# One layer of a hybrid decoder on one Trainium2 core: the output projection's weight units in another order, two weight splits and a norm chain moved

## The chip, the cores and the metric

The kernel runs on 1 core of one Trainium2 chip. The metric is device time in microseconds (us). Engines are named as the profile names them: PE is TensorE's matmul and PEld its weight load, DVE is VectorE, ACT is ScalarE, POOL is GpSimd, SP is SyncE, which here only issues loads.

## The reference, cut to what matters

For 512 tokens of width 1024 in float32, one layer does three things, each between two RMS norms:

```
x = x + 0.5 * rms_norm(swiglu(rms_norm(x, ffn1_pre_g), ffn1_w_gu, ffn1_w_down), ffn1_post_g)
y = hybrid_mixer(rms_norm(x, mix_pre_g), w_in, conv_w, ..., w_o)
x = x + rms_norm(y, mix_post_g)
x = x + 0.5 * rms_norm(swiglu(rms_norm(x, ffn2_pre_g), ffn2_w_gu, ffn2_w_down), ffn2_post_g)
```

The mixer ends in the place that the change touches:

```
y_lru  = rg_lru(x_lru, ...) * gelu(gate_lru)            # 512 channels: recurrence
y_attn = sliding_window_sink_attention(q, k, v, sinks)  # 512 channels: attention
y = concatenate([rms_norm(y_lru, g_lru_out), rms_norm(y_attn, g_attn_out)], axis=-1)
return y @ w_o                                          # w_o is 1024 x 1024
```

## The kernel before, in words

**Products in parts.** Each float32 operand is split into a high part (rounded, ACT: `whi`, `yah`, `ylh`) and a low part (the rest, DVE: `wlo`, `yal`, `yll`). A product is high by high, high weight by low operand, and low weight by high operand.

**Order.** The tile framework keeps the order in which the code issues work, engine by engine. It places the waits and chooses the buffers, PSUM banks among them; each engine runs its own list in order.

**Weights.** The class `Weights` holds all weights as units in one order. A raw tile (1 MB, five of them, two held by `x_rows` here) is loaded by SP and holds several units. `W.take` hands out the next unit. `W.fill(n)` makes sure that n units past those taken are split: for each a cast on ACT (L184) and a subtraction on DVE (L189). When a raw tile's last unit is split, the next load is issued. The code that calls `W.fill` thus sets where the casts and splits stand in the two engines' lists. One unit of `w_o`, the pair (6, 1), is split by a `deferred` call earlier on.

**The output projection.** A unit of `w_o` is a pair of contraction chunks (128 channels each) by one half `dh` of the 1024 outputs: (4, 0), (6, 0), (4, 1), (6, 1) for attention and (0, 0), (2, 0), (0, 1), (2, 1) for the recurrence, in that order before. The tokens are four blocks `tb` of 128, each with two PSUM banks, `wo00` to `wo31` (block, half). The attention part comes first, for blocks 0 to 2: `yah0` to `yah3` and `yal0` to `yal3` are the parts of its four channel chunks. They come from the transposes `atp0` to `atp3` (L1577), which stand in PSUM banks too. For n = 0 and 1 only the high operand is multiplied; then come the low ones of both.

**The gating.** In between stand the statistics of the recurrence: `acc_lru`, the sum of squares on DVE, goes through PE (L454), ACT (`rms_slru`) and DVE (`dg_lru`) and is spread by PE (L469). ACT copies it out (`bc`), and for each of four chunks DVE scales `xc`, ACT makes `ylh` and DVE `yll`. Behind them all stand four casts and splits of recurrence weights. PE does the third block of attention and block 3 meanwhile, and then the recurrence part block by block in `boundary`, through `produce(tb, dh)`.

**The boundary.** In `boundary`, `rows.piece` takes the sum of squares of a finished bank (ACT `sqyr`, L602) and multiplies it by the gain (DVE `zr`, L624). `rows.steps` is a block's norm chain, which `advance` takes a step further at a time: DVE adds the sums (`toty`), ACT and DVE invert, DVE adds to `x_rows`, ACT squares (`sqxr`), DVE adds (`totx`), and so on to the normed `xn`, which PE transposes into `tp_r` (L650). Between these, `W.fill` splits the first units of the next feed-forward, `bg` and `bu`.

Of the kernel before, what the change touches and what calls it, by code (L numbers as in the profile page):

```python
# [15 lines left out]
P = 128  # L16
T = 512
# [6 lines left out]
KC = C // P  # L24
# [98 lines left out]
def tile_layer(ctx: ExitStack, tc: tile.TileContext, out: bass.AP, **ins: bass.AP):  # L123
    nc = tc.nc
    pe, dve, act, pool, sync = nc.tensor, nc.vector, nc.scalar, nc.gpsimd, nc.sync
# [15 lines left out]
    def bank(name):  # L141
        return psum.tile([P, T], F32, tag="bank", name=name)

    def t2k(name, dt=F32):
        return big.tile([P, T], dt, tag="t2k", name=name, bufs=NT2K)

    def wt(name, w=T, dt=F32):
        return tmp.tile([P, w], dt, tag="w", name=name, bufs=NW)


    W = Weights()
    w1, w2, w_in, w_o = ins["ffn1_w_gu"], ins["ffn2_w_gu"], ins["w_in"], ins["w_o"]

    def load_raw(srcs, nk, w, name):
        raw = wpool.tile([P, nk * w], F32, tag="raw", name=f"raw_{name}", bufs=NRAW).rearrange("p (k c) -> p k c", k=nk)
        o = 0
        for src in srcs:
            n = src.shape[1]
            sync.dma_start(raw[:, :, o:o + n], src.rearrange("(k p) c -> p k c", p=P))
            o += n  # L160
        return raw
# [16 lines left out]
    def add_unit(r, part, nk, c, name, low=dve):  # L178
        def two(t, like):
            return t.rearrange("p k (i d) -> p k i d", i=2) if len(like.shape) == 4 else t  # L180

        def cast(raw):
            x, (hi, lo) = part(raw), w_tiles(nk, c, name)
            act.copy(two(hi, x), x)  # L184
            return hi, lo

        def take_low(raw, hi, lo):
            x = part(raw)
            low.tensor_sub(two(lo, x), x, two(hi.bitcast(F32), x))  # L189

        W.unit(r, cast, take_low)
# [132 lines left out]
    for c in (0, 2):  # L324
        for add in add_cols(w_in, KC + c, KD, "gt"):
            add()
    WO = [(k, dh) for k0 in (KC, 0) for dh in range(2) for k in (k0, k0 + 2)]
    for k0 in (KC, 0):
        for dh in range(2):
            r = W.raw(lambda k0=k0, dh=dh: load_raw([w_o[0, k0 * P:(k0 + 4) * P, dh * T:(dh + 1) * T]], 4, T, f"wo{k0}{dh}"))  # L330
            for i in (0, 2):
                add_unit(r, lambda raw, i=i: raw[:, i:i + 2, :], 2, T, f"wo{k0 + i}{dh}", deferred if (k0 + i, dh) == (KC + 2, 1) else dve)
    GROUPS2 = [(0, 6), (6, 10), (10, 14), (14, 18), (18, 22)]
    add_layer(w2, ins["ffn2_w_down"], "b", GROUPS2, CLASSIC2, SEVEN_DOWN2, 0)
# [14 lines left out]
    for i in range(2):  # L349
        load_x(0, i)  # L350
        for o in (0, F):
            r = first_raw[o, i] = t2k(f"first{o}{i}").rearrange("p (k c) -> p k c", k=4)
# [43 lines left out]
    def col(name, i):  # L396
        return colrange(name)[:, i:i + 1]
# [24 lines left out]
    def k_high(ws, banks, xs, sl, ks):  # L422


        for k in ks:
            xh = xs[k][0][:, sl]
            for (hi, lo), ps in zip(ws, banks):
                pe.matmul(ps[:, sl], hi[:, k, :], xh, start=k == 0, stop=False)
                pe.matmul(ps[:, sl], lo[:, k, :], xh, start=False, stop=False)

    def k_low(ws, banks, xs, sl):
        n = len(xs)
        for (hi, lo), ps in zip(ws, banks):
            for k in range(n):
                pe.matmul(ps[:, sl], hi[:, k, :], xs[k][1][:, sl], start=False, stop=k == n - 1)


    def square(src, sl, name, scale=1.0):
# [40 lines left out]
    def x_high(x, src, gain, sl):  # L479
        act.activation(x[0][:, sl], src, AF.Copy, scale=gain)  # L480
# [175 lines left out]
    def boundary(rows, produce, parts, turns, fills, ahead, name):  # L656


        nxt = rows.nxt
        lower, upper = range(4), range(4, KD)  # L660
        chain = iter(())

        def advance(n):
            for _ in range(n):
                next(chain, None)

        for tb in range(NB - 1):
            for dh in range(2):
                ps = produce(tb, dh)
                for t in turns.get((tb, dh), ()):  # L670
                    rows.turn(t)
                W.fill(fills.get((tb, dh), 0))
                if dh == 0:
                    advance(3)
                rows.piece(tb, dh, ps, parts and parts[tb, dh])
            chain = rows.steps(tb)
            if tb < NB - 2:
                advance(ahead)
        ps = [produce(NB - 1, dh) for dh in range(2)]
        advance(1)  # L680
        rows.turned(nxt.high, 0, lower)
        advance(1)
        rows.turned(nxt.low, 0, lower)
        W.cast(1)
        rows.turned(nxt.high, 0, upper)
        advance(1)
        rows.turned(nxt.low, 0, upper)
        W.fill(2)
        advance(1)
        for dh in range(2):  # L690
            rows.piece(NB - 1, dh, ps[dh], parts and parts[NB - 1, dh])
        if nxt.xg:
            rows.turned(nxt.keep, 0, range(KD))
        xs, (l, r) = nxt.xs, HALF
        W.cast(4)
        ws, banks = [], []

        def one(n, part, xpart, stop=False):
            for w, b in zip(ws[n:], banks[n:]):
                for k in range(KD):  # L700
                    pe.matmul(b[:, l], w[part][:, k, :], xs[k][xpart][:, l], start=k + part + xpart == 0, stop=stop and k == KD - 1)  # L701

        def more():
            ws.extend(W.take(0) for _ in range(2))
            banks.extend(bank(f"{name}n{len(banks)}") for _ in range(2))

        more()
        one(0, 0, 0)
        one(0, 0, 1)
        one(0, 1, 0, True)  # L710
        chain = rows.steps(NB - 1)
        advance(4)
        W.fill(2)
        rows.turn(2)
        more()
        one(2, 0, 0)
        one(2, 0, 1)
        rows.turn(3)
        for cs in (lower, upper):
            rows.turned(nxt.high, 1, cs)  # L720
            rows.turned(nxt.low, 1, cs)
        if nxt.xg:
            rows.turned(nxt.keep, 1, range(KD))
        one(2, 1, 0, True)
        W.fill(2)
        k_high(ws, banks, xs, r, range(KD))
        k_low(ws, banks, xs, r)
        return banks

# [279 lines left out]
    banks = [bank(f"a_first{i}") for i in range(4)]  # L1009
# [228 lines left out]
    def produce(tb, dh):  # L1238
        if dh == 0:
            last_banks[tb] = [bank(f"yal{tb}{i}") for i in range(2)]  # L1240
        if tb or not dh:
            for i, f in last.steps(tb, (dh,) if tb else (0, 1)):
                mm3_out(last_banks[tb][i], hs[f - f0], tb, last.weights(f, i), f % 2, ALL, f == f0, f == f1 - 1)
        if (tb, dh) == (0, 1):
            split_gates()
        return last_banks[tb][dh]
# [56 lines left out]
    k0 = const.tile([P, P], F32, name="k0")  # L1303
# [309 lines left out]
    rows2 = Rows("r2", x_rows, "mix_post_g", 1.0 / D, eps, n2)  # L1613
    wo_banks, wo = [], {}
# [10 lines left out]
    def wo_bank(tb):  # L1625
        wo_banks.append([bank(f"wo{tb}{dh}") for dh in range(2)])

    for tb in range(NB - 1):
        wo_bank(tb)
    for n, (k0, dh) in enumerate(WO[:4]):  # L1630
        wo[k0, dh] = W.take(0)
        for xp in ((0,), (0,), (0, 1), (0, 1))[n]:
            for tb in range(NB - 1):
                wo_product(tb, dh, k0, k0 == KC, False, (xp,))
        if n == 1:
            W.fill(2)
            for k0, dh in WO[:2]:
                for tb in range(NB - 1):
                    wo_product(tb, dh, k0, False, False, (1,))
            for l in lrms:  # L1640
                l.stats()
        if n == 2:
            bc = wt("bc")
            for l, sl in zip(lrms, HALF):
                act.copy(bc[:, sl], l.spread())
            for ci in range(KC):
                dve.tensor_mul(hl[ci], hl[ci], bc)
                y = t2k(f"ylh{ci}", F32R), t2k(f"yll{ci}", F32R)
                x_high(y, hl[ci], col("g_lru_out", ci), ALL)
                x_low(y, hl[ci], col("g_lru_out", ci), ALL)  # L1650
                ysp[ci] = y
            W.fill(3)
    wo_bank(NB - 1)
    for k0, dh in WO[:4]:
        wo_product(NB - 1, dh, k0, k0 == KC, False)
    W.fill(4)

    def produce(tb, dh):
        for k0 in (0, 2):
            if (k0, dh) not in wo:  # L1660
                wo[k0, dh] = W.take(0)
            wo_product(tb, dh, k0, False, k0 == 2)
        return wo_banks[tb][dh]

    banks = boundary(rows2, produce, None, {(2, 0): [0], (2, 1): [1]}, {(0, 1): 1, (1, 0): 2}, 2, "m")

    x_hbm = hbm.tile([T, D], F32, name="x_hbm")
    for tb in range(NB):
# [20 lines left out]
    for tb in range(NB):  # L1689
        end = tb == NB - 1  # L1690
        pieces = [(0, 0, T)] + ([(1, 0, T // 2), (1, T // 2, T)] if end else [(1, 0, T)])
        banks = [bank(f"ybl{tb}{i}") for i in range(len(pieces))]
# [3 lines left out]
        for i, f in last.steps(tb, range(len(pieces))):  # L1696
            dh, c0, c1 = pieces[i]
# [17 lines left out]
        rs = small.tile([P, 1], F32, tag="rs1", name=f"rs_b{tb}")  # L1715
# [34 lines left out]
```

## Time and profile before

| | us |
|---|---|
| median of 3 runs (865.73 to 866.11) | 865.96 |
| the profiled execution | 866.93 |
| its span, first to last instruction | 865.0 |
| PE busy | 853.3 |
| DVE busy | 652.7 |
| ACT busy | 529.8 |

The profiled execution is 1.93 us longer than its span, and 0.97 above the median of the runs. The mean clock granted to TensorE is 0.997 of full speed. In the span, the output projection runs from 465 to 516 us.

A row of the timeline gives the start, the length, the engine, the line, the operation with output and inputs, the shape, how often it stands there, and in brackets how long the engine had been idle before it and what ended that. Several alike are one row, whose length then covers them all. Rows of before have the lines of the code shown above.

### The profile page before, as it was taken

How to read it: one execution, taken by the hardware profiler on the slowest of the kernel's cores; microseconds unless marked ns; L12 is line 12 of the kernel's file. 1: busy time of each engine (PE TensorE's matmuls, PEld its weight loads, DVE VectorE, ACT ScalarE, POOL GpSimd, SP SyncE). 2: the span in 40 equal slices, each digit the busy share in tenths (PEclk: the TensorE clock that was granted, in tenths of full speed). 3: DMA queues.
4: the chain of work that ended last, by engine and by line, in shares of the span. 5: the costliest groups of instructions: out<-in, count | busy, mean ns of one | idle time of the engine just before them, and what ended most of it. 6: DMA issues, size and time to landing. Idle time of an engine off the chain costs nothing.

```text
span 865.0 us, 14200 instructions
## 1 busy us (share of the span) xinstructions
PE 853.3 (99%) x5554; PEld 778.3 (90%) x5554; DVE 652.7 (75%) x894; ACT 529.8 (61%) x905; POOL 168.1 (19%) x202
## 2 busy tenths in 40 slices
PE   8999999999999999999999999999999999999996
PEld 8988999989989998998787779888999998998995
DVE  4988897887898866855688675456589798889856
ACT  6647567566576564755787476335456666657552
POOL 2022005013034011013354021001001402303402
PEclk9999999999999999999999999999999999999999
DMA  8265339739469363143211118235323955938922
GB/s 245 99 195 195 128 106 229 196 95 237 132 122 282 125 216 98 54 142 98 87 37 49 51 48 292 75 119 197 126 90 101 236 155 132 233 99 187 262 89 97
DMA packets 92866, 124.42 MB, mean 144 GB/s; under 512 B 5824, under 2 KB 62464, under 8 KB 92800
## 3 DMA queue, kind: packets, MB, share of 16 engines
q1 hardware_dynamic: 76240, 86.68, 31.8%
q0 software_dynamic: 16416, 36.71, 19.1%
q8 instruction: 43, 0.70, 0.3%
q14 instruction: 23, 0.19, 0.1%
q10 hardware_dynamic: 144, 0.13, 0.0%
HBM read 93.10 MB, written 30.41 MB: 143 GB/s over the span
## 4 chain that ended last, share of the span: by engine, by line
PE 92%; DVE 3%; ACT 2%; POOL 1%; DMA 1%; issue 1%; SPq 0%; DVEq 0%; ACTq 0%
PE aa L819 12%; PE ab L819 11%; PE da L819 6%; PE db L819 5%; PE ba L819 3%; PE bb L819 3%; PE wo L1623 2%; PE a_first L1014 2%; PE mn L701 1%; PE an L701 1%; PE yal L1148 1%; PE yal L1146 1%; PE yb L1148 1%; PE yb L1147 1%; PE yal L1147 1%; PE yb L1146 1%
## 5 line engine op out<-in xcount | busy, mean ns | idle before, releaser
L927 POOL DMA_DIRECT2D yp_b<-stage x42 | 36.5, 1115 | 149.1 <-ACT stage L924 140.3
L927 POOL DMA_DIRECT2D yp_a<-stage x42 | 37.0, 1126 | 146.2 <-ACT stage L924 141.1
L1175 POOL DMA_DIRECT2D yp_b<-stage x8 | 4.3, 541 | 91.8 <-ACT stage L1174 91.0
L1146 PE MATMUL yal<-whi_ad,hha 128*128 128x512 f32 x48 | 18.9, 393 | 0.0
L1148 PE MATMUL yal<-whi_ad,hla 128*128 128x512 f32 x48 | 18.7, 390 | 0.0
L1147 PE MATMUL yal<-wlo_ad,hha 128*128 128x512 f32 x48 | 18.7, 389 | 0.0
L1146 PE MATMUL yb<-whi_bd,hhb 128*128 128x512 f32 x48 | 18.7, 389 | 0.0
L1147 PE MATMUL yb<-wlo_bd,hhb 128*128 128x512 f32 x48 | 18.7, 389 | 0.0
L1148 PE MATMUL yb<-whi_bd,hlb 128*128 128x512 f32 x48 | 18.7, 389 | 0.0
L189 DVE TENSOR_TENSOR wlo_bd<-raw_bd,whi_bd 128x1024 fp32r<-128x1024 f32 x10 | 12.1, 1223 | 8.1 <-ACT whi_bd L184 8.1
L1297 POOL TENSOR_TENSOR xcl<-xc,xch 128x512 fp32r<-128x512 f32 x4 | 6.3, 1570 | 57.1 <-ACT xch L1296 57.1
L189 DVE TENSOR_TENSOR wlo_ad<-raw_ad,whi_ad 128x1024 fp32r<-128x1024 f32 x10 | 12.2, 1221 | 4.0 <-ACT whi_ad L184 4.0
L552 POOL TENSOR_TENSOR xg_f<-xh_f,xl_f 128x256 f32<-128x256 f32 x8 | 5.8, 760 | 46.6 <-DVE xl_f L483 46.6
L409 PE MATMUL gt<-xh_mx,whi_gt 128*128 128x512 f32 x32 | 14.2, 443 | 0.0
L1623 PE MATMUL wo<-whi_wo,yah 128*128 128x512 f32 x32 | 13.1, 410 | 0.8 <-ACT yah L480 0.8
L602 ACT ACTIVATE sqxr<-x_rows 128x512 f32<-128x512 f32 x16 | 10.0, 631 | 5.7 <-DVE x_rows L632 5.7
L1623 PE MATMUL wo<-wlo_wo,ylh 128*128 128x512 f32 x32 | 12.6, 393 | 0.8 <-DVE wlo_wo L189 0.8
L1147 PE MATMUL ybl<-wlo_bd,hhb 128*128 128x512 f32 (+1 forms) x36 | 13.2, 366 | 0.0
L1146 PE MATMUL ybl<-whi_bd,hhb 128*128 128x512 f32 (+1 forms) x36 | 13.2, 366 | 0.0
L1148 PE MATMUL ybl<-whi_bd,hlb 128*128 128x512 f32 (+1 forms) x36 | 13.2, 365 | 0.0
L1709 POOL TENSOR_TENSOR yp_b<-yp_b,grow 128x512 f32<-128x512 f32 x6 | 7.7, 1290 | 27.2 <-ACT ysq L1702 27.2
L1702 ACT ACTIVATE ysq<-yp_b 128x512 f32<-128x512 f32 (+1 forms) x9 | 5.2, 583 | 12.4 <-DVE yp_b L1701 11.7
(1845 smaller groups left out, 3726.5 us busy)
## 6 DMA issues: line engine op xcount, KB each, us to landing
yp_a<-stage POOLq DMA_DIRECT2D x50, 256.0 KB, 7.2
yp_b<-stage POOLq DMA_DIRECT2D x50, 256.0 KB, 8.0
raw_ad<-in_ffn_w_down SPq DMA_DIRECT2D x4, 1024.0 KB
raw_wo<-in_w_o SPq DMA_DIRECT2D x4, 1024.0 KB, 5.1
raw_bd<-in_ffn_w_down SPq DMA_DIRECT2D x4, 1024.0 KB
xn<-in_x SPq DMA_DIRECT2D x8, 256.0 KB, 3.6
x_rows<-in_x POOLq DMA_DIRECT2D x4, 512.0 KB, 12.2
yp_a<-yp_a POOLq DMA_DIRECT2D x8, 256.0 KB, 9.2
```

The costliest lines, as they stand in the source:

```text
L189: low.tensor_sub(two(lo, x), x, two(hi.bitcast(F32), x))
L409: pe.matmul(ps, hi[:, k, :], xh, start=start, stop=False)
L602: act.activation(wt(f"sq{name}{self.name}{tb}{dh}"), src, AF.Square, accum_out=self.ss[name, tb][:, dh:dh + 1])
L701: pe.matmul(b[:, l], w[part][:, k, :], xs[k][xpart][:, l], start=k + part + xpart == 0, stop=stop and k == KD - 1)
L819: pe.matmul(o, w[:, k, js], x, start=first and i + j + k == 0, stop=k == 3 and i == 2, skip_group_check=True)
L927: pool.dma_start(o, st.rearrange("p (a b) -> p a b", a=2) if len(o.shape) == 3 else st, accum_op=ALU.add)
L1014: pe.matmul(banks[j][:, HALF[0]], ws[j][part][:, k, :], n1.xs[k][xpart][:, HALF[0]], start=k == 0 and part == xpart, stop=stop and k == KD ...
L1146: pe.matmul(ps, hh[:, blk], hi[:, k, cs], start=start, stop=False)
L1147: pe.matmul(ps, hh[:, blk], lo[:, k, cs], start=False, stop=False)
L1148: pe.matmul(ps, hl_[:, blk], hi[:, k, cs], start=False, stop=stop)
L1623: pe.matmul(wo_banks[tb][dh], x, w[:, k, :], start=start and k == 0 and w is hi and not xp, stop=stop and k == 1 and xp == 1)
L1709: pool.tensor_mul(y, y, grow[dh][:, c0:c1])
```

## The change

Four things. The units of `w_o` go by pairs of chunks and then by halves: (4, 0), (4, 1), (6, 0), (6, 1), (0, 0), (0, 1), (2, 0), (2, 1). The two units split behind the gating at n = 2 are split ahead of it, behind the statistics at n = 1. In `boundary`, the fill follows `advance` and `rows.piece`, and the first fill is that of (0, 0) instead of (0, 1). And in `k_high` and `k_low` the first matmul of a second half no longer carries the start flag.

```diff
-    WO = [(k, dh) for k0 in (KC, 0) for dh in range(2) for k in (k0, k0 + 2)]
+    WO = [(k, dh) for k in (KC, KC + 2, 0, 2) for dh in range(2)]
     for k0 in (KC, 0):
-        for dh in range(2):
-            r = W.raw(lambda k0=k0, dh=dh: load_raw([w_o[0, k0 * P:(k0 + 4) * P, dh * T:(dh + 1) * T]], 4, T, f"wo{k0}{dh}"))
-            for i in (0, 2):
+        rs = [W.raw(lambda k0=k0, dh=dh: load_raw([w_o[0, k0 * P:(k0 + 4) * P, dh * T:(dh + 1) * T]], 4, T, f"wo{k0}{dh}")) for dh in range(2)]
+        for i in (0, 2):
+            for dh, r in enumerate(rs):
                 add_unit(r, lambda raw, i=i: raw[:, i:i + 2, :], 2, T, f"wo{k0 + i}{dh}", deferred if (k0 + i, dh) == (KC + 2, 1) else dve)
...
             for (hi, lo), ps in zip(ws, banks):
-                pe.matmul(ps[:, sl], hi[:, k, :], xh, start=k == 0, stop=False)
-                pe.matmul(ps[:, sl], lo[:, k, :], xh, start=False, stop=False)
+                for w in (hi, lo):
+                    pe.matmul(ps[:, sl], w[:, k, :], xh, start=False, stop=False, skip_group_check=True)
...
-                W.fill(fills.get((tb, dh), 0))
                 if dh == 0:
                     advance(3)
                 rows.piece(tb, dh, ps, parts and parts[tb, dh])
+                W.fill(fills.get((tb, dh), 0))
...
             for l in lrms:
                 l.stats()
+            W.fill(4)
         if n == 2:
...
                 ysp[ci] = y
-            W.fill(3)
...
-    banks = boundary(rows2, produce, None, {(2, 0): [0], (2, 1): [1]}, {(0, 1): 1, (1, 0): 2}, 2, "m")
+    banks = boundary(rows2, produce, None, {(2, 0): [0], (2, 1): [1]}, {(0, 0): 2, (1, 0): 2}, 2, "m")
```

On PE, at the end of the first pass of attention (the four rows for block 2 of unit (4, 0)) and into the second, before. `whi_wo40` is the high part of unit (4, 0), and the brackets name the engine that a row waits for:

```order
L1623 MATMUL wo20_5312<-whi_wo40_4601,yah0_5228 128x512 [waits PE_49]
L1623 MATMUL wo20_5312<-wlo_wo40_4602,yah0_5228 128x512
L1623 MATMUL wo20_5312<-whi_wo40_4601,yah1_5235 128x512
L1623 MATMUL wo20_5312<-wlo_wo40_4602,yah1_5235 128x512
L1623 MATMUL wo00_5308<-whi_wo60_4761,yah2_5246 128x512 [waits Activation_49]
L1623 MATMUL wo00_5308<-wlo_wo60_4762,yah2_5246 128x512
L1623 MATMUL wo00_5308<-whi_wo60_4761,yah3_5254 128x512 [waits Activation_49]
```

And after:

```order
L1623 MATMUL wo20_5312<-whi_wo40_4601,yah0_5228 128x512 [waits PE_49]
L1623 MATMUL wo20_5312<-wlo_wo40_4602,yah0_5228 128x512
L1623 MATMUL wo20_5312<-whi_wo40_4601,yah1_5235 128x512
L1623 MATMUL wo20_5312<-wlo_wo40_4602,yah1_5235 128x512
L1623 MATMUL wo01_5309<-whi_wo41_4761,yah0_5228 128x512 [waits DVE_49]
L1623 MATMUL wo01_5309<-wlo_wo41_4762,yah0_5228 128x512
L1623 MATMUL wo01_5309<-whi_wo41_4761,yah1_5235 128x512
L1623 MATMUL wo01_5309<-wlo_wo41_4762,yah1_5235 128x512
L1623 MATMUL wo11_5311<-whi_wo41_4761,yah0_5228 128x512 [waits DVE_49]
```

The second pass now reads `yah0` and `yah1` again and writes the banks of the other half; its waits for ACT give way to waits for DVE, which has read those banks.

On DVE, from the statistics to the recurrence part, before:

```order
L465 TENSOR_SCALAR dg_lru1_5367<-ident_119,rs_lru1_5365 128x128 x2
L1647 TENSOR_TENSOR xc0_4361<-xc0_4361,bc_5388 128x512
L483 SCALAR_TENSOR_TENSOR yll0_5395<-xc0_4361,cols_136,ylh0_5394 128x512
...
L483 SCALAR_TENSOR_TENSOR yll3_5410<-xc3_4422,cols_136,ylh3_5409 128x512
L189 TENSOR_TENSOR wlo_wo00_5414<-raw_wo00_4765,whi_wo00_5413 128x1024
L189 TENSOR_TENSOR wlo_wo20_5418<-raw_wo00_4765,whi_wo20_5417 128x1024
L189 TENSOR_TENSOR wlo_wo01_5468<-raw_wo01_5096,whi_wo01_5467 128x1024
L189 TENSOR_TENSOR wlo_wo21_5472<-raw_wo01_5096,whi_wo21_5471 128x1024
```

And after:

```order
L465 TENSOR_SCALAR dg_lru1_5367<-ident_119,rs_lru1_5365 128x128 x2
L189 TENSOR_TENSOR wlo_wo00_5371<-raw_wo00_4894,whi_wo00_5370 128x1024
L189 TENSOR_TENSOR wlo_wo01_5375<-raw_wo01_5096,whi_wo01_5374 128x1024
L1648 TENSOR_TENSOR xc0_4361<-xc0_4361,bc_5396 128x512
...
L483 SCALAR_TENSOR_TENSOR yll3_5418<-xc3_4422,cols_136,ylh3_5417 128x512
L189 TENSOR_TENSOR wlo_wo20_5466<-raw_wo00_4894,whi_wo20_5465 128x1024
L189 TENSOR_TENSOR wlo_wo21_5472<-raw_wo01_5096,whi_wo21_5471 128x1024
```

Two splits, and on ACT their casts, stand ahead of the gating, two behind it; the units are (0, 0) and (0, 1) first, then (2, 0) and (2, 1).

On DVE in `boundary`, from block 0's last addition to `x_rows` to block 1's second `zr`, before:

```order
L632 SCALAR_TENSOR_TENSOR x_rows0_2971<-zr201_5516,rs1y_r20_5513,x_rows0_2971 128x512
L189 TENSOR_TENSOR wlo_bu0_0_5539<-raw_bu0__5475,whi_bu0_0_5538 128x1024
L608 TENSOR_TENSOR totx_r20_5542<-ssx_r20_5520 128x1
L611 RECIPROCAL rs1x_r20_5543<-rs1x_r20_5543 128x1
L642 TENSOR_SCALAR xn_r200_5547<-x_rows0_2971,rs1x_r20_5543 128x512
L624 TENSOR_TENSOR zr210_5554<-wo10_5310,grow_r20_5304 128x512
L608 TENSOR_TENSOR toty_r21_5570<-ssy_r21_5551 128x1
L624 TENSOR_TENSOR zr211_5574<-wo11_5311,grow_r21_5305 128x512
```

And after:

```order
L632 SCALAR_TENSOR_TENSOR x_rows0_2971<-zr201_5516,rs1y_r20_5513,x_rows0_2971 128x512
L608 TENSOR_TENSOR totx_r20_5538<-ssx_r20_5520 128x1
L611 RECIPROCAL rs1x_r20_5539<-rs1x_r20_5539 128x1
L642 TENSOR_SCALAR xn_r200_5543<-x_rows0_2971,rs1x_r20_5539 128x512
L624 TENSOR_TENSOR zr210_5550<-wo10_5310,grow_r20_5304 128x512
L189 TENSOR_TENSOR wlo_bu0_0_5553<-raw_bu0__5475,whi_bu0_0_5552 128x1024
L608 TENSOR_TENSOR toty_r21_5570<-ssy_r21_5547 128x1
L624 TENSOR_TENSOR zr211_5574<-wo11_5311,grow_r21_5305 128x512
```

The split of `bu` has moved behind block 0's whole chain and block 1's first `zr`, and on ACT its cast has moved in the same way, from behind `sqxr` to between block 1's two `sqyr`.

More of the change, by code (lines that the diff above doesn't have):

```diff
@@ L434, in k_low @@
             for k in range(n):
-                pe.matmul(ps[:, sl], hi[:, k, :], xs[k][1][:, sl], start=False, stop=k == n - 1)
+                pe.matmul(ps[:, sl], hi[:, k, :], xs[k][1][:, sl], start=False, stop=k == n - 1, skip_group_check=True)
     def square(src, sl, name, scale=1.0):
@@ L1659, in produce @@
         for k0 in (0, 2):
-            if (k0, dh) not in wo:
-                wo[k0, dh] = W.take(0)
+            while (k0, dh) not in wo:
+                wo[WO[len(wo)]] = W.take(0)
             wo_product(tb, dh, k0, False, k0 == 2)
         return wo_banks[tb][dh]
-    banks = boundary(rows2, produce, None, {(2, 0): [0], (2, 1): [1]}, {(0, 1): 1, (1, 0): 2}, 2, "m")
+    banks = boundary(rows2, produce, None, {(2, 0): [0], (2, 1): [1]}, {(0, 0): 2, (1, 0): 2}, 2, "m")
     x_hbm = hbm.tile([T, D], F32, name="x_hbm")
```

## The prediction

> **What bounds the kernel now.** I read the page's shares first, then all waits of TensorE (PE), then the stretch that the change touches, engine by engine.
>
> ```profile
> PE 853.3 (99%) x5554; PEld 778.3 (90%) x5554; DVE 652.7 (75%) x894; ACT 529.8 (61%) x905; POOL 168.1 (19%) x202
> ```
>
> PE is busy for 853.3 of 865.0 us. The change adds and removes no matmul, so it can only close gaps of PE. All its waits by what ended them (sum, times, longest; left out is one of 0.2 at 456 us), and the busy time of the three stretches that hold those of `wo` and `tp_r` (columns: length, then PE, PEld, DVE, ACT, POOL busy, granted clock, DMA):
>
> ```profile
> PE warm L1001 <- POOL ident masks.py:199: 1.4, 1, 1.4
> PE wo L1623 <- ACT yah L480: 0.8, 2, 0.4
> PE a_first L1014 <- ACT xh_a L480: 0.8, 1, 0.8
> PE wo L1623 <- DVE wlo_wo L189: 0.8, 1, 0.8
> PE tp_r L650 <- DVE zr L624: 0.4, 2, 0.2
> PE tp_r L650 <- DVE xn_r L642: 0.3, 1, 0.3
> ...
> 465.40:475.10 9.70, 8.91 (x40) 6.74 (x39) 7.96 (x11) 8.35 (x14) 2.36 (x2) 1.00 0.00 1
> 490.50:504.90 14.40, 13.64 (x60) 11.09 (x60) 10.67 (x15) 8.92 (x17) 0.00 (x0) 1.00 0.45 146
> 504.90:511.00 6.10, 5.33 (x30) 3.88 (x29) 3.65 (x9) 4.18 (x14) 0.00 (x0) 1.00 0.01 3
> ```
>
> Gaps here: 0.79 + 0.76 + 0.77 = 2.32 us, at a full clock. The first and third wait of the list are the kernel's start; behind 511 us there is none. A gap costs more than its idle time, since a matmul's 0.39 us overlaps the next one; the loss is the distance between starts less the usual step. Everything that the change can win lies here.
>
> **Part 1: w_o's units by pairs of contraction chunks (term 1).** As it stands, the second pass needs `yah2` and `yah3`, which ScalarE (ACT) gives late:
>
> ```profile
> 468.02 0.39 PE L1623 MATMUL wo<-wlo_wo,yah 128*128 128x512 f32 x1
> 468.84 0.50 PE L1623 MATMUL wo<-whi_wo,yah 128*128 128x512 f32 x1 [0.42 <-ACT yah L480]
> 469.94 0.50 PE L1623 MATMUL wo<-whi_wo,yah 128*128 128x512 f32 x1 [0.37 <-ACT yah L480]
> 470.27 0.40 PE L1623 MATMUL wo<-wlo_wo,yah 128*128 128x512 f32 x1
> 472.36 2.88 PE L1623 MATMUL wo<-whi_wo,yal 128*128 128x512 f32 x12
> 475.08 0.95 PE L454 MATMUL rms_lru<-mean_c,acc_lru 128*128 128x1 f32 x8
> 468.23 2.71 DVE L483 SCALAR_TENSOR_TENSOR yal<-atp,cols,yah 128x512 fp32r<-128x512 f32 x4
> 472.06 2.27 DVE L1598 TENSOR_TENSOR acc_lru<-acc_lru,sq_l 128x512 f32<-128x512 f32 x3
> ```
>
> The step is (475.08 - 472.36)/12 = 0.227 us. From 468.02 to 470.27 are four steps, 0.91 us; they took 2.25, so the two waits cost 1.34. After the change the second pass uses `yah0` and `yah1` again, there since 465.4. The twelve matmuls from 468.25, and then twelve on `yal0` and `yal1`, would end at 468.25 + 24 x 0.227 = 473.7. Two waits are new.
>
> First, the second pass writes the dh = 1 banks earlier. In the built program its three waits are for the copy of `gt3`, for `yal0` and for `yal1`, which read these banks. The four `yal` steps take 2.71 us, 0.68 each: `yal0` ends at 468.9, `yal1` at 469.6, and the banks are wanted at 469.2 and 470.1. No cost, by 0.2 us at the narrowest.
>
> Second, the statistics matmuls L454 now meet VectorE (DVE): the sum `acc_lru` ends at 472.06 + 2.27 = 474.33, behind DVE work that no edit moves. PE starts some 0.06 later (as 468.84 and 469.94 follow their ACT steps), at 474.39 instead of 475.08. **Term 1: -0.69**, half of the 1.34; what is late next is `acc_lru`. Ends: 0 and -1.34.
>
> The order of units also frees the raw tiles otherwise: the fourth load of `w_o` takes the first one's place and so starts behind the third unit's split instead of the second's. Both stand among the attention scores, and the load is wanted only behind the statistics at 475. No cost.
>
> **Part 2: recurrence weights split ahead of the gating (term 2).** As it stands, four casts and four splits stand behind the gating:
>
> ```profile
> 490.54 0.42 PE L1623 MATMUL wo<-whi_wo,ylh 128*128 128x512 f32 x1
> 491.72 0.50 PE L1623 MATMUL wo<-wlo_wo,ylh 128*128 128x512 f32 x1 [0.76 <-DVE wlo_wo L189]
> 492.05 0.40 PE L1623 MATMUL wo<-whi_wo,ylh 128*128 128x512 f32 x1
> 489.37 3.88 ACT L184 CAST whi_wo<-raw_wo 128x1024 fp32r<-128x1024 f32 x4
> 490.44 4.63 DVE L189 TENSOR_TENSOR wlo_wo<-raw_wo,whi_wo 128x1024 fp32r<-128x1024 f32 x4 [0.19 <-ACT whi_wo L184]
> ```
>
> Two steps took 1.51 us instead of 0.45: 1.06 lost. Two casts (3.88/4 = 0.97 each) and two splits (4.63/4 = 1.16 each) move ahead, to where both engines sit idle:
>
> ```profile
> 476.70 0.48 DVE L465 TENSOR_SCALAR dg_lru<-ident,rs_lru 128x128 f32<-128x128 f32 x2
> 480.74 0.81 ACT L1645 COPY bc<-rms_lru 128x256 f32<-128x256 f32 x2 [4.42 <-PE rms_lru L469]
> 481.58 0.69 DVE L1647 TENSOR_TENSOR xc<-xc,bc 128x512 f32<-128x512 f32 x1 [4.39 <-ACT bc L1645]
> ```
>
> ACT has 4.42 us of cover for 1.9 of work, and DVE 4.39 for 2.3 (with the first cast ahead of it, 3.3). All three rows come 0.69 earlier after term 1, so the cover stays. Were it gone, `bc` would be late by what is lacking, and PE's wait at 490.5 with it. The gating then ends as far ahead of PE as now, and behind it stand two casts and splits, no longer four. The first now serves (2, 0), which PE reaches 6 steps = 1.36 us after 490.54, its low part at 492.1 by today's clock; it is ready at 490.44 + 1.2 = 491.7. The margin is 0.45 us, the thinnest here. **Term 2: -1.06.** Ends: 0 (the wait comes back in another place) and -1.06.
>
> **Part 3: block 0's norm chain ahead of the gate-up split `bu` (term 3).**
>
> ```profile
> 500.94 0.19 ACT L602 ACTIVATION_READ_ACCUMULATOR sqxr<-x_rows 128x1 f32 x1
> 501.03 1.03 ACT L184 CAST whi_bu<-raw_bu__5475 128x1024 fp32r<-128x1024 f32 x1
> 503.95 0.73 ACT L640 ACTIVATE xn_r<-x_rows,rs1x_r 128x512 f32<-128x512 f32 x1 [0.23 <-DVE rs1x_r L611]
> 504.58 0.58 ACT L602 ACTIVATE sqyr<-wo 128x512 f32<-128x512 f32 x1
> 505.15 0.59 ACT L602 ACTIVATE sqyr<-wo 128x512 f32<-128x512 f32 x1
> 502.10 1.23 DVE L189 TENSOR_TENSOR wlo_bu<-raw_bu__5475,whi_bu 128x1024 fp32r<-128x1024 f32 x1 [1.79 <-ACT whi_bu L184]
> 503.24 0.15 DVE L608 TENSOR_TENSOR totx_r<-ssx_r 128x1 f32<-128x1 f32 x1
> 505.28 0.69 DVE L624 TENSOR_TENSOR zr<-wo,grow_r 128x512 f32<-128x512 f32 x1 [0.85 <-ACT sqyr L602]
> 505.96 0.68 DVE L624 TENSOR_TENSOR zr<-wo,grow_r 128x512 f32<-128x512 f32 x1
> 506.03 0.44 PE L650 MATMUL tp_r<-ident,xn_r 128*128 128x128 f32 x2 [0.21 <-DVE zr L624]
> 506.70 0.44 PE L650 MATMUL tp_r<-ident,xn_r 128*128 128x128 f32 x2 [0.23 <-DVE zr L624]
> ```
>
> The transposes wait for banks that block 1's two `zr` read, and these stand behind block 0's chain, which waits for the cast and split of `bu`. By today's clock, after the change: `totx` at 501.17 (not 503.24), `xn` 0.71 later at 501.88, `sqyr` 0.63 later at 502.51, the first `zr` 0.70 later at 503.21. But `bu` now stands ahead of the second `zr`: its cast at 502.51 + 0.57 = 503.08, its split 1.07 later at 504.15, the next DVE step 1.14 after that at 505.29, and the second `zr` at 505.36, against 505.96. **Term 3: -0.60**: of the two waits the first goes, the second shrinks. Block 1's own chain starts from that `zr`, so it and PE move together and the 0.33 us wait for `xn` stays. Ends: 0, and -1.1 if that goes too.
>
> Moving the fill for `bg` from (0, 1) to (0, 0) leaves both engines' rows where they were. The feed-forward's loads, which wait on SP for raw tiles, start earlier or as now.
>
> **Part 4: no start flag on the second half's first matmul.** It stands in the rows as any other:
>
> ```profile
> 529.89 0.28 PE L428 MATMUL mn<-xh_f,whi_bg 128*128 128x256 f32 x1
> 530.01 0.28 PE L429 MATMUL mn<-xh_f,wlo_bg 128*128 128x256 f32 x1
> ```
>
> The first has the flag, the second not: 0.28 each. Cost 0; twelve matmuls lose the flag, so even a whole step of 0.12 each would be 1.4, either way; I take 0, as the rows are of the very operation.
>
> **Sum.** -0.69 - 1.06 - 0.60 = -2.35 us. The profiled execution took 866.93 us (span 865.0 and 1.93 around it), 0.97 over the median of 865.96, which I take as a constant offset: 864.6 for it, a span near 862.7, and 863.6 for the median. Behind 511 us PE waits for nothing now, so nothing there gives the gain back. A measurement of this kernel can tell about 0.2% (1.73 us) from no change.
>
> **Rivals.**
>
> *A part only.* The thin margin of term 2 fails and PE waits for (2, 0)'s low part, or the second `zr` comes no earlier. Either takes 0.6 to 1.06 away: gain 1.3 to 1.75, near 864.5, within 0.2%. For it: DVE and ACT steps vary by a tenth or two. Against: three tenths are left over.
>
> *The banks.* If the dh = 1 banks came free only behind all four `yal` steps, the second pass would start at 468.23 + 2.71 + 0.06 = 471.0, and the statistics at 471.0 + 24 x 0.227 = 476.45, 1.37 later than now: terms 1 to 3 give 1.37 - 1.06 - 0.60 = -0.3, so 865.7, no change. Against it: the three waits of the built program. [...] No row of before shows it, as the dh = 1 banks are first used after 475.
>
> *Slower: `bu` lands late.* Its cast now stands ahead of block 1's chain on ACT, so each us that its load is late delays the transposes and (2, 1) by one.
>
> ```profile
> 492.82 0.38 SPq L159 DMA_DIRECT2D raw_bu__5475<-in_ffn_w_gu  x1
> ```
>
> It was issued at 492.82 and the cast at 501.03 did not wait, so it landed within 8.2 us. Now it is issued behind one split, at 491.7 - 0.69 = 491.0, and wanted at 503.08 - 1.75 = 501.3, 10.3 us later. It would have to take 12.7 us to eat the whole gain and 14.4 to make the kernel slower by 0.2% (867.7). [...] The rows speak for less.
>
> *More.* If `acc_lru` is ready sooner than PE, or the wait for `xn` goes, up to 0.65 more: 862.9.
>
> **Chances.** Forecast 0.60 (863.0 to 864.2), a part only 0.20, banks 0.08, late `bu` 0.05, more 0.07. Faster by over 0.2% are the forecast, more, and a sliver of a part only: 0.68. Within 0.2%: the rest of a part only and most of banks, 0.26. Slower: late `bu` and a hundredth of banks, 0.06. The range, 862.9 to 865.2, holds the forecast, more and a part only with half a us to spare, and leaves out the other two, 0.13.
>
> **What would show it.** Right: no wait for `yah`; a wait of 0.5 to 0.7 us for `acc_lru` before L454; casts and splits of `wo` between 475 and 479.5; no wait for `wlo_wo`; one wait for `zr` in place of two. Wrong: a wait for `yal` at 469 to 471, `bc` more than 0.7 us behind the spread, a wait for `wlo_wo` two tiles later, or `whi_bu` waiting for its load.

## The result, and the profile after

The changed kernel takes 863.45 us, the median of 8 runs (863.18 to 864.59), against 865.92 for the kernel before in the same comparison (865.62 to 866.63). The ratio is 0.9973, with a 95% interval of 0.9962 to 0.9984: faster by 2.5 us or 0.27%, with 0.16% at the near end of the interval. The forecast was 863.6, in a range of 862.9 to 865.2.

The waits of TensorE (PE) come first, since the change could only close gaps of PE (columns: who waited for whom, sum, times, longest). After:

```profile
PE warm L1001 <- POOL ident masks.py:199: 1.4, 1, 1.4
PE a_first L429 <- ACT xh_a L480: 0.7, 1, 0.7
PE rms_lru L454 <- DVE acc_lru L1598: 0.6, 1, 0.6
PE a_first L1014 <- ACT xh_a L480: 0.4, 1, 0.4
PE xtp L948 <- DMA xn<-in_x: 0.4, 1, 0.4
PE tp_r L650 <- DVE xn_r L642: 0.3, 1, 0.3
```

The waits for `yah`, `wlo_wo` and `zr` are gone, the one for `xn_r` stayed, and a wait of 0.62 us for `acc_lru` is new. That is the list that the prediction gave, but for the one shorter wait for `zr` that it left: it is still there, too short to be listed (third place below). The waits for `a_first` and `xtp` stand in the first 25 us.

Before the gain can be placed, the axis has to be set right. The first product of `w_o` and the first matmul of the feed-forward, in the timeline of before (two rows) and of after (two rows):

```profile
465.43 0.48 PE L1623 MATMUL wo<-whi_wo,yah 128*128 128x512 f32 x1
516.64 1.12 PE L701 MATMUL mn<-xh_f,whi_bg 128*128 128x256 f32 x8
```

```profile
464.34 0.48 PE L1623 MATMUL wo<-whi_wo,yah 128*128 128x512 f32 x1
513.32 1.11 PE L701 MATMUL mn<-xh_f,whi_bg 128*128 128x256 f32 x8
```

After stands 1.09 us earlier at the first of these rows already. From the first row to the second are 51.21 us before and 48.98 after: the change's own part on the trace is -2.23. I call this distance the w_o stretch. Behind it lie 348.36 us to the end of the span before and 348.38 after, so nothing is given back. The 1.09 us are not the change's; what they are is told below, with the last runs.

Where the 2.23 come from is read at three places. First, PE up to the statistics, and the DVE rows that release it:

```profile
469.89 2.88 PE L1623 MATMUL wo<-whi_wo,yal 128*128 128x512 f32 x12
473.39 1.02 PE L454 MATMUL rms_lru<-mean_c,acc_lru 128*128 128x1 f32 x8 [0.62 <-DVE acc_lru L1598]
478.47 1.02 PE L469 MATMUL rms_lru<-dg_lru,ones 128*128 128x256 f32 x4
467.13 2.71 DVE L483 SCALAR_TENSOR_TENSOR yal<-atp,cols,yah 128x512 fp32r<-128x512 f32 x4
470.97 2.27 DVE L1598 TENSOR_TENSOR acc_lru<-acc_lru,sq_l 128x512 f32<-128x512 f32 x3
```

The statistics stand 473.39 - 464.34 = 9.05 us behind the first product, before 475.08 - 465.43 = 9.65: -0.60. The sum `acc_lru` ends at 473.24, 8.90 behind the first product, exactly as before (474.33 - 465.43): DVE is not moved, and PE now waits for it. The spread L469, which starts the gating, stands 14.13 behind, before 14.68 (480.11 - 465.43, the row below): -0.55.

```profile
480.11 1.02 PE L469 MATMUL rms_lru<-dg_lru,ones 128*128 128x256 f32 x4
```

Second, the recurrence weights on ACT and DVE, and the recurrence products on PE:

```profile
474.61 1.99 ACT L184 CAST whi_wo<-raw_wo 128x1024 fp32r<-128x1024 f32 x2
475.69 2.36 DVE L189 TENSOR_TENSOR wlo_wo<-raw_wo,whi_wo 128x1024 fp32r<-128x1024 f32 x2
479.10 0.81 ACT L1646 COPY bc<-rms_lru 128x256 f32<-128x256 f32 x2 [2.50 <-PE rms_lru L469]
488.79 2.36 DVE L189 TENSOR_TENSOR wlo_wo<-raw_wo,whi_wo 128x1024 fp32r<-128x1024 f32 x2 [0.18 <-ACT whi_wo L184]
489.35 0.39 PE L1623 MATMUL wo<-whi_wo,ylh 128*128 128x512 f32 x1
490.49 0.39 PE L1623 MATMUL wo<-wlo_wo,ylh 128*128 128x512 f32 x1
```

Two casts and two splits now stand ahead of `bc`, and ACT is still idle for 2.50 us behind them. The third recurrence product is at 489.35, 25.01 behind the first product of `w_o`, before 26.62: another -1.06. The low part of (2, 0), wanted at 490.49, is ready at 488.79 + 1.18 = 489.97, so the margin that the prediction called the thinnest came out at 0.5 us.

Third, the boundary, DVE, ACT and PE:

```profile
498.45 0.16 DVE L608 TENSOR_TENSOR totx_r<-ssx_r 128x1 f32<-128x1 f32 x1 [0.85 <-ACT sqxr L602]
500.50 0.69 DVE L624 TENSOR_TENSOR zr<-wo,grow_r 128x512 f32<-128x512 f32 x1 [0.84 <-ACT sqyr L602]
501.44 1.23 DVE L189 TENSOR_TENSOR wlo_bu<-raw_bu__5475,whi_bu 128x1024 fp32r<-128x1024 f32 x1 [0.25 <-ACT whi_bu L184]
502.65 0.68 DVE L624 TENSOR_TENSOR zr<-wo,grow_r 128x512 f32<-128x512 f32 x1
500.37 1.04 ACT L184 CAST whi_bu<-raw_bu__5475 128x1024 fp32r<-128x1024 f32 x1
502.50 1.33 PE L650 MATMUL tp_r<-ident,xn_r 128*128 128x128 f32 x8
503.59 0.48 PE L1623 MATMUL wo<-whi_wo,ylh 128*128 128x512 f32 x1
506.92 1.09 PE L650 MATMUL tp_r<-ident,xn_r 128*128 128x128 f32 x8 [0.33 <-DVE xn_r L642]
```

Block 0's chain runs without the split of `bu` in it. The eight transposes are one row, 1.33 long (1.04 in e6 below, where nothing holds them): the last pair still waits a little for the second `zr` at 502.65, which stands behind the split. The first product behind them is at 503.59, 39.25 behind the first product of `w_o`. Before it was 41.46 (the row below): -2.21 up to here, so another -0.60.

```profile
506.89 0.48 PE L1623 MATMUL wo<-whi_wo,ylh 128*128 128x512 f32 x1
```

### The profile page after: what moved, and what is told of

The parts are those of the page before. It is cut to its first block, busy times and chain, and to the rows that moved or that the text cites. A ratio compares the mean times of both kernels' runs of the same rounds, so it can differ in the third digit from the quotient of the medians.

```text
span 861.7 us, 14199 instructions
## 1 busy us (share of the span) xinstructions
PE 850.7 (99%) x5554; PEld 776.6 (90%) x5554; DVE 653.5 (76%) x894; ACT 529.7 (61%) x905; POOL 167.0 (19%) x202
## 4 chain that ended last, share of the span: by engine, by line
PE 91%; DVE 3%; ACT 2%; DMA 1%; POOL 1%; issue 1%; SPq 0%; DVEq 0%; ACTq 0%
PE aa L819 12%; PE ab L819 11%; PE da L819 6%; PE db L819 5%; PE ba L819 3%; PE wo L1623 3%; PE bb L819 3%; PE mn L701 1%; PE an L701 1%; PE yal L1147 1%; PE yal L1148 1%; PE yb L1148 1%; PE yb L1147 1%; PE yal L1146 1%; PE yb L1146 1%; DMA raw_second<-in_ffn_w_gu 1%
## 5 line engine op out<-in xcount | busy, mean ns | idle before, releaser
L1623 PE MATMUL wo<-whi_wo,yah 128*128 128x512 f32 x32 | 12.8, 402 | 0.0
L1623 PE MATMUL wo<-whi_wo,ylh 128*128 128x512 f32 x32 | 12.6, 395 | 0.0
```

What stands on the lines that cost most here:

```text
L1623: pe.matmul(wo_banks[tb][dh], x, w[:, k, :], start=start and k == 0 and w is hi and not xp, stop=stop and k == 1 and xp == 1)
```

## The experiments

All 11 runs are in one table. The w_o stretch is read from each run's timeline, as above; the last column is its change against the base. It repeats to 0.02 us (after, two executions: 48.98 and 48.96), while the medians carry 0.1% of uncertainty, so the stretch is what places a gain and the median is what confirms it. In all 13 profiled executions the part behind the stretch is 348.29 to 348.39 us long.

| kernel | median us | ratio to before (95%) | stretch | against |
|---|---|---|---|---|
| before | 865.92 to 866.07 | 1 | 51.21 | |
| e1 order of units alone | 866.40 | 1.0005 (0.9996, 1.0014) | 51.60 | before +0.39 |
| e2 splits ahead alone | 865.08 | 0.9991 (0.9983, 1.0000) | 50.11 | before -1.10 |
| e3 chain ahead alone | 866.59 | 1.0007 (0.9998, 1.0016) | 51.73 | before +0.52 |
| e9 the same, count mended | 865.50 | 0.9992 (0.9983, 1.0001) | 50.57 | before -0.64 |
| e4 no start flags alone | 865.93 | 0.9999 (0.9990, 1.0007) | 51.22 | before +0.01 |
| after | 863.45 | 0.9973 (0.9962, 0.9984) | 48.98 | before -2.23 |
| e11 after once more | 863.52 | 0.9972 (0.9962, 0.9982) | 48.96 | before -2.25 |
| e10 after, chain as before | 863.99 | 0.9977 (0.9968, 0.9986) | 49.55 | after +0.57 |
| e8 after, yal order 2, 3, 0, 1 | 864.40 | 0.9982 (0.9973, 0.9991) | 50.00 | after +1.02 |
| e5 after, statistics later | 862.72 | 0.9961 (0.9949, 0.9974) | 48.16 | after -0.82 |
| e6 after, bu later | 862.54 | 0.9963 (0.9949, 0.9976) | 48.17 | after -0.81 |
| e7 both of these | 862.20 | 0.9956 (0.9944, 0.9969) | 47.30 | after -1.68 |

**e1, the order alone.** Before, with the new order, the loads listed to match it as in the change, and `produce` taking the units in that order (the last four lines, which are part of the change too):

```diff
-    WO = [(k, dh) for k0 in (KC, 0) for dh in range(2) for k in (k0, k0 + 2)]
+    WO = [(k, dh) for k in (KC, KC + 2, 0, 2) for dh in range(2)]
...
-            if (k0, dh) not in wo:
-                wo[k0, dh] = W.take(0)
+            while (k0, dh) not in wo:
+                wo[WO[len(wo)]] = W.take(0)
```

> The kernel before with the order of units alone. Theory (first term, as the sum had it): the waits for yah go, PE waits 0.6 for acc_lru, the statistics start 0.6 to 0.7 earlier against the first product of w_o. But the order alone has a price that the whole change hides: behind the gating the splits now go (0, 0), (0, 1), (2, 0), and (2, 0), wanted second, is split third. By 1.16 us for a split, its low part is there at about 493.9 on the axis of before and wanted at 493.1, so a second wlo_wo wait of about 0.8 us, and the sum is -0.65 + 0.8: 866.0, no change. Rival 1 (banks come free only behind all four yal steps): statistics 1.4 us later than in before, a wait for DVE yal, 867.5. Rival 2 (order costs nothing behind the gating): one wlo_wo wait of 0.8, 865.3.

PE and DVE rows of this kernel:

```profile
473.78 1.02 PE L454 MATMUL rms_lru<-mean_c,acc_lru 128*128 128x1 f32 x8 [0.58 <-DVE acc_lru L1598]
489.21 4.63 DVE L189 TENSOR_TENSOR wlo_wo<-raw_wo,whi_wo 128x1024 fp32r<-128x1024 f32 x4 [0.19 <-ACT whi_wo L184]
490.49 0.50 PE L1623 MATMUL wo<-wlo_wo,ylh 128*128 128x512 f32 x1 [0.77 <-DVE wlo_wo L189]
492.76 0.50 PE L1623 MATMUL wo<-wlo_wo,ylh 128*128 128x512 f32 x1 [0.61 <-DVE wlo_wo L189]
```

The first product stands at 464.74 here, so the statistics are at 9.04, as in after: the wait for `acc_lru` is the order's doing, and the banks cost nothing. The second row is the price: four splits behind the gating, with (2, 0) third, and a second wait for `wlo_wo`. The two steps from 491.75 to 493.09 take 1.34 instead of 0.45, and these 0.89 eat the first gain of 0.55. The stretch is 0.39 longer in all, where 0.15 was expected; by the median it is no change, as expected.

**e2, the splits alone.** Before, with `W.fill(4)` behind `l.stats()` and no `W.fill(3)` behind the gating.

> The kernel before with the two recurrence splits ahead of the gating, and nothing else. Theory (second term): the wlo_wo wait of 0.76 goes, (0, 0) and (2, 0) are both there, PE gains 1.06 us from the first recurrence product on; the two yah waits and the two zr waits stay as they were: 864.9. Rival (the splits delay bc and the gating): the wait comes back at ylh and the time stays within 0.3 us of 865.9.

The `wlo_wo` wait is gone, both `yah` waits stand, and so do the two stops of 0.2 us at the transposes (one is put down to `zr`, one to `toty`, the next step on DVE), the stretch is 1.10 shorter and the time 865.08. The second term holds by itself.

**e3 and e9, the chain alone.** In e3, before has the fill behind `rows.piece` and the counts of after; in e9 the first count is 3:

```diff
-                W.fill(fills.get((tb, dh), 0))
                 if dh == 0:
                     advance(3)
                 rows.piece(tb, dh, ps, parts and parts[tb, dh])
+                W.fill(fills.get((tb, dh), 0))
...
-    banks = boundary(..., {(0, 1): 1, (1, 0): 2}, 2, "m")
+    banks = boundary(..., {(0, 0): 2, (1, 0): 2}, 2, "m")   # e3
+    banks = boundary(..., {(0, 0): 3, (1, 0): 2}, 2, "m")   # e9
```

> The kernel before with the fills of boundary behind the norm chain, and nothing else. Theory (third term): the first zr wait goes, the second shrinks, (2, 1) starts 0.6 us earlier against the first recurrence product, the 0.33 wait for xn stays: 865.3. Rival (the split of bu in the new place delays as much as it did in the old one, or its load comes late): 865.9 or above.

e3 went the other way. Its DVE rows between block 1's two `zr`, and the PE row that waits for them:

```profile
502.14 0.69 DVE L624 TENSOR_TENSOR zr<-wo,grow_r 128x512 f32<-128x512 f32 x1 [0.84 <-ACT sqyr L602]
503.08 1.23 DVE L189 TENSOR_TENSOR wlo_bg<-raw_bg__5421,whi_bg 128x1024 fp32r<-128x1024 f32 x1 [0.25 <-ACT whi_bg L184]
504.22 1.22 DVE L189 TENSOR_TENSOR wlo_bu<-raw_bu__5475,whi_bu 128x1024 fp32r<-128x1024 f32 x1
505.43 0.69 DVE L624 TENSOR_TENSOR zr<-wo,grow_r 128x512 f32<-128x512 f32 x1
506.17 0.44 PE L650 MATMUL tp_r<-ident,xn_r 128*128 128x128 f32 x2 [1.21 <-DVE zr L624]
```

Two splits stand there, where after has one. A count in `fills` is relative to the units already taken. With the new order, block 0's first half has taken seven units of `w_o`, and two more reach `bg`; with the old order it has taken six, two more are both `w_o`'s and split already, and `bg` slips behind the first `zr` of block 1. It cost 1.14 us of DVE time and a wait of 1.21. I had missed this when I wrote e3; the new count `(0, 0): 2` belongs to the order of units as much as to the chain.

> The kernel before with the fills of boundary behind the norm chain and the count at (0, 0) raised to 3, so that bg is split there and bu alone stands ahead of the second zr, as in after. Theory (the third term stands by itself; e3_chain failed because with the old order of units its counts put both bg and bu between the two zr): (2, 1) and the feed-forward start 0.6 earlier against the first product of w_o than the 51.2 us of before, 50.6, and 865.4. Rival (the chain's gain needs the other parts of the change): 51.2 or more, 866.

With the count mended, block 1 has only `bu` between the two `zr`, no wait for `zr` is recorded, and the stretch is 0.64 shorter: the third term stands by itself.

**e10, after without the chain.** 

> The kernel after with the fills of boundary as in before, so parts 1, 2 and 4 alone. Theory: the two zr waits of 0.2 are back, from the first product of w_o to the first of the feed-forward 49.0 + 0.6 = 49.6 us, 864.1. Rival (parts 1 and 2 give the whole gain): 49.0, 863.5.

The two `zr` waits are back (0.4 in sum), the stretch is 0.57 longer and the time 863.99. Against before the stretch is 1.66 shorter, so terms 1 and 2 hold together without the chain (-0.55 and -1.06).

**e4, no start flags.** 

> The kernel before without the start flags of the second halves. Theory: no row changes, 865.9, and the first product of w_o stands where it does in the trace of before or up to 1.2 us earlier by the granted clock of the first 20 us alone (0.87 to 0.96 in the profiled execution of before, 1.00 in that of after, where it stands 1.09 earlier). Rival: the flags are what brings that product 1.09 us earlier, 864.8, in every execution and at an equal clock.

51.22 against 51.21, and 865.93 against 866.06: nothing. The first product stands at 464.77, 0.66 earlier than in before, at a granted clock of 1.00 in the first 20 us. That is within what the theory left to the clock, and since the median did not fall, the flags are not what starts `w_o` early.

**e8, the banks.** After, with the `x_low` steps in the order 2, 3, 0, 1.

> The kernel after, with the four low parts of attention in the order 2, 3, 0, 1, so that the banks which the second pass writes are read last. It asks how near the first term was to the rival of the banks. Theory (each bank of the second pass waits for the one yal step that reads it): yal0 ends 1.36 later, at 469.2 instead of 467.8, and the second block of the pass, wanted at 468.07, waits about 1.1 us for DVE yal; the third then finds yal1 there or waits 0.1 more. The statistics follow at 472.6 + 1.2 = 473.8 instead of 473.39, since 0.7 of it is taken from the wait for acc_lru: 863.9. Rival (no wait for the banks at all, they are guarded otherwise): 863.45 and no wait for yal.

PE (line 1621 is L1623 of after) and DVE:

```profile
468.86 0.50 PE L1621 MATMUL wo<-whi_wo,yah 128*128 128x512 f32 x1 [0.30 <-DVE yal L483]
469.95 0.50 PE L1621 MATMUL wo<-whi_wo,yah 128*128 128x512 f32 x1
468.05 0.75 DVE L483 SCALAR_TENSOR_TENSOR yal<-atp,cols,yah 128x512 fp32r<-128x512 f32 x1 [0.51 <-ACT yah L480]
469.15 2.07 DVE L483 SCALAR_TENSOR_TENSOR yal<-atp,cols,yah 128x512 fp32r<-128x512 f32 x3 [0.35 <-ACT yah L480]
472.33 2.28 DVE L1596 TENSOR_TENSOR acc_lru<-acc_lru,sq_l 128x512 f32<-128x512 f32 x3
```

The loss was twice what I wrote (0.95 us over after's median where I had 0.45), and it came by another way. PE starts the second and third block of the pass at 468.86 and 469.95, behind the ends of the first two `yal` steps (468.80 and about 469.84) and not behind all four (471.22). The first two steps are now `yal2` and `yal3`, so in this run the two blocks have the banks of `atp2` and `atp3`, not of `atp0` and `atp1` as I had assumed. It fits banks that are handed out in the order in which they come free. So each bank waits for the one step that reads it, and the rival of the banks is refuted at that place, as in after itself: there these blocks start at 468.07 and 468.99, ahead of the end of the four steps at 469.84. The 1.02 on the stretch are DVE's: it idles 0.51 + 0.35 for `yah2` and `yah3`, `acc_lru` ends 1.0 later (474.61, that is 9.94 behind the first product at 464.67, against 8.90), and PE waits for it again.

**e5, e6 and e7, what is late next.** e5 puts the statistics four matmuls further on, behind the third unit's first block (the count of the fill is 3 there, since one more unit is taken); e6 moves the second fill of `boundary`; e7 does both.

```diff
-            for l in lrms:
-                l.stats()
-            W.fill(4)
...
             for tb in range(NB - 1):
                 wo_product(tb, dh, k0, k0 == KC, False, (xp,))
+                if (n, xp, tb) == (2, 0, 0):
+                    for l in lrms:
+                        l.stats()
+                    W.fill(3)
...
-    banks = boundary(..., {(0, 0): 2, (1, 0): 2}, 2, "m")
+    banks = boundary(..., {(0, 0): 2, (2, 0): 2}, 2, "m")
```

> The kernel after, with the statistics (L454) four matmuls later, behind the third unit's first block. Theory (acc_lru is what comes last there, and nothing behind it is bound): PE's wait of 0.62 for acc_lru goes and a step of refill with it, the spread and all behind it stand 0.6 to 0.8 earlier, 862.75. Rival (the gating, 0.3 us later at its start, becomes the bound): a wait for ylh or wlo_wo of that size, 863.1 to 863.5.

> The kernel after, with the split of bu behind (2, 0) and so behind block 1's zr and norm chain. Theory (the split is what still holds the second zr and xn): the last pair of transposes of tp_r no longer waits 0.24, the wait for xn of 0.33 goes, 0.55 to 0.65 gained, 862.85; bu, wanted at 518, is there in time. Rival 1 (xn is bound by the zr and squares alone): only 0.24 gained, 863.2. Rival 2 (cast and split now hold xh_f, which the feed-forward wants at 513.3): a wait for xh_f, 863.5 or above.

> Both of the last two at once, the version that should beat before and after. Theory: the gains add, 0.7 + 0.6, 862.15 and no wait of PE between 465 and 540. Rival (one takes from the other, or a new wait behind 511): 862.8 or above.

All waits of PE in e7:

```profile
PE warm L1001 <- POOL ident masks.py:199: 1.4, 1, 1.4
PE a_first L429 <- ACT xh_a L480: 0.7, 1, 0.7
PE xtp L948 <- DMA xn<-in_x: 0.3, 1, 0.3
PE po L1501 <- POOL pa L1488: 0.3, 1, 0.3
```

None is listed from 465 us on, and e7 is the best version, 862.20 us, below before (0.9956, 0.9944 to 0.9969) and 1.25 below after's median. Each listed wait that went gave about 0.2 more than its idle time: e5 0.82 for a wait of 0.62; in e6 the way from block 0's transposes to behind block 1's is 0.54 shorter for a wait of 0.33 (503.59 to 507.77 in after, 503.20 to 506.84 in e6), and block 0's transposes take 0.29 less. That is the rule of the prediction's first part (a matmul's 0.39 us overlaps the next one at a step of 0.227, 0.16 of it lost at each stop), which I did not apply fully when I sized e6. On the stretch the two add up: 0.82 + 0.81 against 1.68.

**e11, after once more.** 

> The kernel after once more, beside the two above. Theory: 863.5, 49.0 us from the first product of w_o to the first of the feed-forward, the one wait for acc_lru and the one for xn. Its first product of w_o may stand anywhere from 464.2 to 465.4, by the waits and the clock of the first 30 us; if it stood at 464.3 whenever the order is that of after, part of the gain would lie ahead of w_o.

The first product stands at 465.59 here, later than in before, and the stretch is 48.96. So the early start is no part of the change: the four other runs with the old order have it at 464.37 to 464.92, the seven others with the new one at 464.21 to 465.16. What sets before and this run apart (465.43 and 465.59) stands in the first 15 us (columns: window, its length, busy time of PE, PEld, DVE, ACT, POOL, granted clock, DMA share, GB/s). Three windows here, and then the middle one in before and in the first profile of after:

```profile
8.00:10.00 2.00, 1.52 (x7) 1.13 (x7) 1.52 (x4) 0.46 (x1) 0.00 (x0) 0.78 1.13 331
10.00:12.00 2.00, 2.00 (x11) 2.00 (x10) 1.01 (x3) 1.86 (x4) 0.00 (x0) 0.50 1.21 291
12.00:14.00 2.00, 2.00 (x17) 2.00 (x16) 2.00 (x6) 1.06 (x1) 1.61 (x1) 0.86 1.13 328
```

```profile
10.00:12.00 2.00, 2.00 (x11) 2.00 (x11) 1.54 (x4) 1.78 (x4) 0.13 (x1) 0.50 1.22 290
10.00:12.00 2.00, 2.00 (x19) 2.00 (x18) 2.00 (x6) 1.41 (x4) 0.50 (x1) 1.00 1.20 289
```

What spreads the other eleven over 0.95 us no run shows.

## Why the prediction was right

**The axis.** It made the sum against the profiled execution and took that one's 0.97 us over the median as a constant offset: 864.6 for such an execution, a span near 862.7. The profile of after has 863.36 and 861.7. The offset was not constant. The profiled execution of before had the half clock shown for e11 (0.81, 0.50 and 0.84 in the same three windows), the first one of after had not; e11, which had it, has 864.63 and 862.9. The forecast for the median is untouched, since the offset was taken off again. That it came within 0.15 us of the median is in part luck: on the stretch the sum was 0.12 too large, and the medians fell by about 0.25 more than the stretch.

**Term 1, -0.69: right mechanism, a little too large.** Both new waits came as named: none for the banks, one for `acc_lru`. Measured is -0.60 at the statistics and -0.55 at the spread. PE started 0.15 behind `acc_lru` (473.39 against 473.24), not 0.06, and the statistics, now behind a stop, took 1.02 instead of 0.95. The prediction had said that a gap costs more than its idle time, but did not count that for the new wait; without the wait (e5) the stretch is 0.82 shorter, for 0.62 of idle time. The margin at the banks, put at 0.2, was 0.26: the first `yal` step ends at 467.13 + 0.68 = 467.81, and its bank is written at 468.07.

**Term 2, -1.06: exact.** -1.06 behind the spread in after, -1.10 alone in e2. The margin for (2, 0) was 0.5, put at 0.45. The prediction called it the thinnest, but its own margin at the banks was thinner.

**Term 3, -0.60: exact.** The recurrence stands 1.61 earlier behind the first product, the transposes' end and all behind it 2.21 to 2.23: -0.60; alone -0.64 (e9), and undone +0.57 (e10). The steps came where it put them: on its clock (2.70 later than in after, by the third recurrence product) the first `zr`, the split of `bu` and the second `zr` stand at 503.20, 504.14 and 505.35, forecast 503.21, 504.15 and 505.36. The wait for `xn` stayed, as it said. The cast of `bu` did not wait for its load, issued at 490.05 and used at 500.37. No run has a load that lands late, so what that rival would cost stays untried.

**Part 4, 0:** 0.01 in e4.

**What the sum hid.** The terms were sized for the whole change, and there they hold: -0.55, -1.06 and -0.60 are -2.21 of the 2.23 measured. They are not the parts' worth each by itself. Alone the parts give +0.39, -1.10, -0.64 and +0.01, together -1.34; the 0.89 that is missing is the second `wlo_wo` wait of e1, which the order brings and the early splits take away. The prediction saw that place only as a thin margin of 0.45.

**What stays open.** The medians differ by 2.47 and 2.52, the stretch by 2.23 and 2.25. The quarter of a us between them is well inside the interval (0.9962 to 0.9984 is 1.4 to 3.3 us), and the scatter of the first product (464.2 to 465.6 over 13 executions) is large enough for it; no run settles it.

## What to carry to other kernels

When a wait is taken away, look up what the engine meets next and size the gain up to there: the order's 1.34 us of waits were worth 0.55, because PE then waited 0.62 for `acc_lru`. A reordering is worth what the whole list makes of it: alone it cost 0.39 us here, since it put a wanted unit third in another engine's list, and a count relative to what is taken (as in `fills`) changes its meaning with the order. For a change of 0.3%, measure a stretch of the trace between two fixed rows around the change; here it repeated to 0.02 us where executions differ by 1.4.

## What the runs showed of the hardware

I had not expected a stretch of half clock in some executions of the same program. In 2 of 13 profiles (one of before, one of after) TensorE's granted clock was 0.50 from 10 to 12 us and 0.78 to 0.86 in the windows on both sides; the other 11 show 1.00 there. In e11, by an estimate from the clocks of these three windows, that is 2 x (0.22 + 0.50 + 0.14) = 1.72 us of full-speed time lost, or 3.4 us at half the rate; in before, windows of half a us show 0.50 from 9.5 to 12.5, with 0.75 and 0.84 on the two sides. Not all of it shows behind: the stop of 0.46 to 0.71 us for `xh_a` at 23 us, which the other eleven have, is absent in these two.

What lowered the clock no run shows. The longest wait of PE listed ahead of it is the 1.4 us at the start, and the first profile of after, at 1.00 in these windows, lists the same 1.4.
